# An unused 160-byte tile moves the expert stage's token tiles to the split weights' address modulo 512

## The chip, the cores and the metric

The kernel runs on one core of one Trainium2 chip. The metric is the device time of one execution in microseconds; the time before is the median of three runs. A core has 128 partitions of on-chip memory (SBUF), in which a tile has one byte address that holds for all partitions, and accumulators in PSUM. TensorE multiplies a stationary operand of 128x128, which a weight load (PEld in the profile) brings in, with a moving operand of up to 512 columns. VectorE is DVE in the profile, ScalarE ACT, SyncE SP; SyncE issues the loads from memory.

## The reference, cut to what matters

A decoder trunk of two layers over 256 tokens of width 1024, all in float32: a pooling mixer and a dense SwiGLU, then an attention mixer with shared keys and values and a mixture of experts, then a norm. The time is mostly in the mixture of experts. Every token goes to two of eight experts; each expert is a SwiGLU of hidden width 3584:

```python
hn = rmsnorm(h, ffn_norm[l])
logits = (hn @ w_router)
top_val, top_idx = lax.top_k(logits, 2)
gates = jax.nn.softmax(top_val, axis=-1)
# for each expert e, over the tokens x that chose it:
h_e = jax.nn.silu(x @ w_gate[e]) * (x @ w_up[e])      # 1024 -> 3584
y_e = h_e @ w_down[e]                                 # 3584 -> 1024
# y[token] += gate * y_e ; out = rmsnorm(h + y)
```

Three weight matrices of 1024 x 3584 float32 for each of eight experts, 352 MB in all, pass once through the core.

## The kernel before

**Precision by splitting.** TensorE multiplies in the reduced type float32r. Each operand is therefore split into a high part (a copy rounded by ScalarE, line 177) and a low part (the difference, by VectorE, line 181), and a product takes three matmuls: high weights with high tokens, high weights with low tokens (line 189), low weights with high tokens (line 192). `mm3` (lines 184 to 192) issues them, for several rows of 128 first all that use the high weights, then those with the low weights.

**Steps.** The work is a list of steps that `run()` (line 236) goes through. A step takes a piece of 128x1024 of a raw weight tile; `split_ahead` splits the pieces of the next three steps before a step's matmuls are issued. The high parts and the low parts have rings of four tiles of 4096 bytes each (`whp`, `wlp`), the raw tiles a ring of 11 tiles of 8192 bytes (`rawp`), to which in the last stage six slots in memory of finished stages are added (lines 751, 768, 770). A raw tile holds two pieces; `load` (line 156) issues its transfer of 1 MB on SyncE's queue as soon as its slot is free.

**Expert stage.** For each expert, `new_slots` (line 987) takes from the pool `m1` the tiles `xeH` and `xeL` (4096 bytes a partition each): the high and low parts of up to 128 of the expert's tokens, transposed, filled by `gather` (line 999) through a matmul with a one-hot. `expert` (line 1045) runs seven blocks of 512 hidden columns: four steps for gate, four for up, and, two blocks late, four steps for down. In a step (`moe_unit`, line 1024) the token tile is the stationary operand, 128x128, and the split weights are the moving operand, 512 columns: six matmuls, each with its own weight load. The hidden block is transposed (line 1054) and split into `hid` (three tiles of 4096 bytes in `m1`), which is the stationary operand of the down steps. After the last block the result goes back to the tokens by a matmul with the one-hot `ohT` (`scatter`, line 1065).

**Output projection.** In the attention stage `out_proj` (line 661) and `w_mm` (line 829) multiply with `w_o` in the same way: `oh` and `ol`, the merged heads transposed, are stationary, 128x128, and 512 columns of split weights are moving, again six matmuls in the order of `mm3`.

**Addresses.** Pools are laid out one after another, a tile's size is rounded up to 32 bytes. The pools on the left side end with those of the attention; `mp` (token tile `xm`, routing tiles of 64 bytes) and below it `m1` grow downwards from the top of the partition. The addresses in bytes, from the program as it is allocated: the four high weight tiles at 96032 and on by 4096, the low ones at 112416 and on, which is 288 modulo 512, as are all raw tiles; `oh` and `ol` of the output projection at 200480 and 202528, also 288 modulo 512; in `m1` `oh` 192960, `xeH` 193984, `xeL` 198080, `hid` 205248, 209344 and 213440, all 448 modulo 512, since each size in that pool is a multiple of 512; `xm` at 220608, also 448. The attention's largest tile ends at 192288, where `m1` would begin to collide. The pieces that a matmul reads lie at multiples of 512 bytes (stationary) or 2048 (moving) in their tiles, so a whole tile keeps one address modulo 512.

The order of the matmuls, loads and splits is that of the steps, written out; nothing in it depends on addresses, except that a tile waits for the tiles that had its memory before.

Of the kernel before, what the change touches and what calls it, by code (L numbers as in the profile page):

```python
# [12 lines left out]
F32 = mybir.dt.float32  # L13
# [24 lines left out]
P = 128  # L38
# [5 lines left out]
FE = 3584  # L44
NB = FE // 512
LAG = 2
EPS = 1e-6
NEG = -1e30
WINDOWS = (2, 4, 8, 16)
# [45 lines left out]
def trunk(ctx, tc, x, a_norm, a_proj, a_scale, kv_norm, w_kv, b_norm, w_q, w_o, rel_bias,  # L95
# [29 lines left out]
    def bankB(name):  # L125
        return psB.tile([P, 512], F32, tag="b", name=name)
# [20 lines left out]
    def flush():  # L147
        while pending:
            tick()
# [51 lines left out]
    def then(fn):  # L201
        steps.append((None, None, None, fn, None))
# [22 lines left out]
    def split_ahead(want):  # L225
        m = flow["now"]
        while m < len(steps) and want >= 0:
            raw_of, cut, name = steps[m][:3]
            if raw_of is not None:
                if m >= flow["reach"]:  # L230
                    flow["parts"][m] = split(cut(raw_of()), name) if name else (cut(raw_of()),)
                    flow["reach"] = m + 1
                want -= 1
            m += 1
# [38 lines left out]
    def rstd_of(ss, name):  # L273
        w = ss.shape[1]
        v = small.tile([P, 2], F32, tag="rv", name=f"rv_{name}")
        nc.vector.tensor_scalar(v[:, :w], ss, 1.0 / D, EPS, op0=ALU.mult, op1=ALU.add)
        r = cst.tile([P, 2], F32, name=f"rstd_{name}")
# [357 lines left out]
    def attend(b, h, i, prT, o):  # L635
        for s, (g, kt) in enumerate(SEG_KEYS[i]):
            nc.tensor.matmul(o, prT[:, s * P:(s + 1) * P], kvT["v", g][:, kt, h * 64:(h + 1) * 64],
                             start=(s == 0), stop=(s == 3))

    def merged(sm, on, i, pu):  # L640
        nc.vector.reciprocal(sm[:, i, :], sm[:, i, :])
        nc.vector.tensor_mul(on[:, i], pu.rearrange("p (h d) -> p h d", h=4),
                             sm[:, i, :].unsqueeze(2).to_broadcast([P, 4, 64]))

    def merge_tiles(b, pool):
        on = pool.tile([P, 2, 4, 64], F32, tag="on", name=f"on{b}")
        oh = pool.tile([P, 2, T], F32R, tag="oh", name=f"oh{b}")
        ol = pool.tile([P, 2, T], F32R, tag="ol", name=f"ol{b}")
        return on, oh, ol

    def turn_merged(b, on, oh, ol, i):
        po = bankB(f"ps_oT{b}_{i}")
        uf = on[:, i].rearrange("p h d -> p (h d)")
        for j in range(2):
            nc.tensor.transpose(po[:, j * P:(j + 1) * P], uf[:, j * P:(j + 1) * P], ident)
        pov = po[:, :T].rearrange("p (j t) -> p j t", j=2)
        hi = oh[:, :, i * P:(i + 1) * P]
        nc.scalar.activation(hi, pov, AF.Copy)
        nc.vector.tensor_sub(ol[:, :, i * P:(i + 1) * P], pov, hi.bitcast(F32))
# [136 lines left out]
    def moe_pool(name, bufs, side, ctx=mo_ctx):  # L796
        return ctx.enter_context(tc.tile_pool(name=name, bufs=bufs, side=side, reuse_waits="tile"))

    def last_merge():
        flush()  # L800
        split_ahead(3)
        pU = [bankB(f"ps_U3_{i}") for i in range(2)]
        on, oh, ol = mo["o"] = merge_tiles(3, av["one"])

        def att(h, i):
            attend(3, h, i, prev["probs"][h, i], pU[i][:, h * 64:(h + 1) * 64])

        for h in range(4):
            att(h, 0)
        merged(prev["sm"], on, 0, pU[0][:, :T])  # L810
        for h in range(3):
            att(h, 1)
        turn_merged(3, on, oh, ol, 0)
        att(3, 1)
        merged(prev["sm"], on, 1, pU[1][:, :T])
        late_ctx.close()
        mp = mo["mp"] = moe_pool("mp", 1, "right")
        mo["xm"] = mp.tile([P, 2, D], F32, name="xm")
        mo["ss"] = mp.tile([P, 2, 2], F32, name="ss_m")
        for nm in ("sel", "both", "gat", "pos"):  # L820
            mo[nm] = mp.tile([P, 2, NE], F32, name=nm)
        spare = av["big"][:, 4096:]
        mo["grow"], mo["sq"] = spare[:, :D], spare[:, D:D + 512]
        mo["h2T"] = {(n, i): av["at"].tile([P, 4, P], F32, tag="lg", name=f"h2T{n}_{i}", bufs=4)
                     for n in range(2) for i in range(2)}

    then(last_merge)

    def w_mm(wh, wl, n, i):
# [215 lines left out]
    def expert(e, got, sfx, next_expert=None):  # L1045
# [31 lines left out]
        def hidden_block(b):  # L1077
            nm = f"{sfx}{e}_{b}"
            ps = {}

            def acc(w):
                def f():
                    if w not in ps:
                        ps[w] = bankA(f"ps_m{w}{nm}")
                    return ps[w]
                return f

            def gate_done():
                hs = ps["h"] = mo["m1"].tile([P, 512], F32, tag=f"hs{b % 2}", name=f"hs{nm}")
                nc.scalar.activation(hs, ps["g"], AF.Silu)  # L1090

            def up_done():
                nc.vector.tensor_mul(ps["h"], ps["h"], ps["u"])
                later(TL if b == NB - 1 and next_expert is None else TURN, lambda: turn_hidden(ps["h"], b))

            for w, src, fn in (("g", moe_gate, gate_done), ("u", moe_up, up_done)):
                for kh in range(2):
                    moe_unit(src[e, kh * 512:(kh + 1) * 512, b * 512:(b + 1) * 512], acc(w),
                             lambda: (got()[1], got()[2]), 4 * kh, kh == 0, kh == 1, f"m{w}{nm}_{kh}",
                             fn if kh == 1 else None)  # L1100
# [10 lines left out]
        def down_unit(b, n):  # L1111
            def acc():
                if n not in hid:
                    hid[n] = psC.tile([P, 512], F32, tag="a", name=f"ps_y{sfx}{e}_{n}")
                return hid[n]

            src = moe_down[e, b * 512:(b + 1) * 512, n * 512:(n + 1) * 512]
            name = f"md{sfx}{e}_{n}_{b}"
            post = (lambda: y_done(n)) if b == NB - 1 else None
            if b in full:  # L1120
                native_unit(src, acc, lambda: hidden[b], b == NB - 1, name, post)
            else:
                moe_unit(src, acc, lambda: hidden[b], 0, b == 0, b == NB - 1, name, post)

        for b in range(NB):
            hidden_block(b)
            if b >= LAG:
                for n in range(2):
                    down_unit(b - LAG, n)
        if next_expert is not None:  # L1130
            then(next_expert)
        rest = [(b, n) for b in range(NB - LAG, NB) for n in range(2)]
        if next_expert is None:
# [5 lines left out]
    def square_out(n, i):  # L1139
# [5 lines left out]
        if n == 0:  # L1145
            nc.gpsimd.tensor_scalar(mo["part"][:, i:i + 1], mo["sso"][:, 0, i:i + 1], 1.0 / D, EPS,
                                    op0=ALU.mult, op1=ALU.add)
# [96 lines left out]
```

## Time and profile before

| | |
|---|---|
| median of three runs | 1567.74 us |
| the runs | 1566.62, 1567.74, 1570.31 us |
| span of the profiled execution | 1566.3 us (its own time beyond the span isn't listed; the fastest run is 1566.62 us) |
| granted clock, mean | 0.995 |
| busy: TensorE, VectorE, ScalarE | 98%, 76%, 64% |
| moved from and to memory | 441 MB, 282 GB/s over the span |

The profile is of one execution. Matmuls overlap, so the duration of one (some 395 ns with 512 columns) is longer than the distance to the next; the distance is read from the starts in the timeline, or from the number of matmuls in a window that is full. The timeline merges instructions of one kind that follow each other into one row with a count. The expert stage's steps begin near 542 us and end near 1552 us; the output projections run at 331, 408 and 484 us, with 24 matmuls each, and in smaller groups at 524 to 531 us.

### The profile page before, as it was taken

The numbers are of one execution on the slowest core, as the hardware profiler recorded it, in microseconds if no ns is written. First come the engines' busy times: TensorE is split into PE (matmuls) and PEld (weight loads), VectorE is DVE, ScalarE is ACT, GpSimd is POOL, SyncE is SP. The second block draws the span as 40 slices with busy tenths as digits, with TensorE's granted clock in tenths as the row PEclk, the third lists the DMA queues.
The fourth block names the chain that finished last, engine by engine and source line by source line (L and its number), as shares of the span: only waits on it lengthen the run. The fifth ranks groups of instructions, "written<-read, shape, count | busy, mean of one in ns | idle before, by whom it ended". The sixth has DMA issues, their size and how long they took to land. (4 is left out here: it accounts for less than half of the span.)

```text
span 1566.3 us, 22560 instructions
## 1 busy us (share of the span) xinstructions
PE 1541.6 (98%) x8849; PEld 1335.6 (85%) x8849; DVE 1198.2 (76%) x1346; ACT 1007.2 (64%) x1206; POOL 9.0 (1%) x16
## 2 busy tenths in 40 slices
PE   8999999999999999999999999999999999999996
PEld 7999999999999988888888888888888888888884
DVE  6666565354545598899888889888889888888984
ACT  5444445444444577777777767777777777777773
POOL 0000000000000000000000000000000000000001
PEclk9999999999999999999999999999999999999998
DMA  9955685646463799999989999999999999999930
GB/s 301 310 168 174 191 213 163 168 135 168 135 170 134 276 353 368 368 314 372 365 312 363 360 331 349 367 334 349 353 362 330 360 366 323 351 372 323 365 120 29
DMA packets 274803, 441.08 MB, mean 282 GB/s; under 512 B 28720, under 2 KB 100656, under 8 KB 274688
## 3 DMA queue, kind: packets, MB, share of 16 engines
q1 hardware_dynamic: 252448, 433.11, 79.6%
q10 hardware_dynamic: 22240, 6.45, 2.9%
q8 instruction: 71, 1.16, 0.3%
q14 instruction: 44, 0.36, 0.1%
HBM read 438.36 MB, written 1.17 MB: 281 GB/s over the span
## 5 line engine op out<-in xcount | busy, mean ns | idle before, releaser
L181 DVE TENSOR_TENSOR wl_mu<-raw_mu,wh_mu 128x1024 fp32r<-128x1024 f32 x196 | 233.2, 1220 | 41.0 <-ACT wh_mu L177 41.0
L181 DVE TENSOR_TENSOR wl_mg<-raw_mg,wh_mg 128x1024 fp32r<-128x1024 f32 x204 | 244.0, 1221 | 14.9 <-ACT wh_mg L177 13.8
L189 PE MATMUL ps_y<-wh_md,hid 128*128 128x512 f32 x880 | 242.7, 397 | 0.0
L177 ACT ACTIVATE wh_mg<-raw_mg 128x1024 fp32r<-128x1024 f32 x204 | 213.3, 1059 | 38.6 <-PE ps_y L189 24.6
L181 DVE TENSOR_TENSOR wl_md<-raw_md,wh_md 128x1024 fp32r<-128x1024 f32 x190 | 223.1, 1219 | 1.0 <-ACT wh_md L177 1.0
L177 ACT ACTIVATE wh_mu<-raw_mu 128x1024 fp32r<-128x1024 f32 x196 | 204.0, 1056 | 23.2 <-PE ps_mg L189 20.7
L177 ACT ACTIVATE wh_md<-raw_md 128x1024 fp32r<-128x1024 f32 x190 | 195.4, 1057 | 29.7 <-PE ps_mu L189 19.2
L189 PEld LDWEIGHTS ps_y<-wh_md,hid 128*128 128x128 f32 x880 | 164.1, 188 | 38.8 <-issue 0.5
L189 PE MATMUL ps_mg<-wh_mg,xeH 128*128 128x512 f32 x448 | 180.7, 403 | 0.0
L189 PE MATMUL ps_mu<-wh_mu,xeH 128*128 128x512 f32 x448 | 178.7, 399 | 0.0
L189 PE MATMUL ps_mg<-wh_mg,xeL 128*128 128x512 f32 x448 | 176.8, 395 | 0.0
L189 PE MATMUL ps_mu<-wh_mu,xeL 128*128 128x512 f32 x448 | 176.5, 394 | 0.0
L192 PE MATMUL ps_mu<-wl_mu,xeH 128*128 128x512 f32 x448 | 140.7, 395 | 0.0
L192 PE MATMUL ps_mg<-wl_mg,xeH 128*128 128x512 f32 x448 | 140.5, 394 | 0.0
L192 PE MATMUL ps_y<-wl_md,hid 128*128 128x512 f32 x440 | 137.9, 394 | 0.0
L192 PEld LDWEIGHTS ps_mu<-wl_mu,xeH 128*128 128x128 f32 x448 | 84.1, 188 | 20.8
L192 PEld LDWEIGHTS ps_mg<-wl_mg,xeH 128*128 128x128 f32 x448 | 84.1, 188 | 20.7
L189 PEld LDWEIGHTS ps_mu<-wh_mu,xeL 128*128 128x128 f32 x448 | 84.1, 188 | 19.6
L189 PEld LDWEIGHTS ps_mu<-wh_mu,xeH 128*128 128x128 f32 x448 | 84.1, 188 | 19.5
L189 PEld LDWEIGHTS ps_mg<-wh_mg,xeL 128*128 128x128 f32 x448 | 84.2, 188 | 18.5
L192 PEld LDWEIGHTS ps_y<-wl_md,hid 128*128 128x128 f32 x440 | 82.6, 188 | 20.4
L189 PEld LDWEIGHTS ps_mg<-wh_mg,xeH 128*128 128x128 f32 x448 | 84.2, 188 | 18.3
(244 smaller groups left out, 2712.6 us busy)
## 6 DMA issues: line engine op xcount, KB each, us to landing
raw_mg<-in_moe_w_gate_dram SPq DMA_DIRECT2D x102, 1024.0 KB, 7.1
raw_mu<-in_moe_w_up_dram SPq DMA_DIRECT2D x98, 1024.0 KB, 6.8
raw_md<-in_moe_w_down_dram SPq DMA_DIRECT2D x96, 1024.0 KB, 7.1
big<-in_moe_w_down_dram SPq DMA_DIRECT2D x16, 1024.0 KB, 7.1
big<-in_moe_w_up_dram SPq DMA_DIRECT2D x14, 1024.0 KB, 6.5
raw_k<-in_w_kv_dram SPq DMA_DIRECT2D x12, 1024.0 KB, 5.3
raw_q<-in_w_q_dram SPq DMA_DIRECT2D x12, 1024.0 KB, 5.5
raw_v<-in_w_kv_dram SPq DMA_DIRECT2D x12, 1024.0 KB, 5.3
```

The lines of the kernel that those rows point to most:

```text
L177: nc.scalar.activation(hv, raw, AF.Copy)
L181: nc.vector.tensor_sub(lv, raw, hv.bitcast(F32))
L189: nc.tensor.matmul(o, a, b, start=start and k == 0 and m == 0, stop=False)
L192: nc.tensor.matmul(o, a, b, start=False, stop=stop and k == n - 1)
```

## The change

A tile of 160 bytes that nothing reads or writes is taken from the pool `mp`, behind the routing tiles. The pool begins 160 bytes lower, and with it `xm` and the whole of `m1`: `xeH` goes from 193984 to 193824, `xeL` to 197920, `hid` to 205088, 209184 and 213280, which is 288 modulo 512, the split weights' own. No other address moves except routing tiles of `mp`, and no instruction is added.

```diff
@@ -44,6 +44,7 @@
 FE = 3584
 NB = FE // 512
 LAG = 2
+PHASE_FILL = 160
 EPS = 1e-6
 NEG = -1e30
 WINDOWS = (2, 4, 8, 16)
@@ -819,6 +820,7 @@
         mo["ss"] = mp.tile([P, 2, 2], F32, name="ss_m")
         for nm in ("sel", "both", "gat", "pos"):
             mo[nm] = mp.tile([P, 2, NE], F32, name=nm)
+        mp.tile([P, PHASE_FILL // 4], F32, name="fill")
         spare = av["big"][:, 4096:]
         mo["grow"], mo["sq"] = spare[:, :D], spare[:, D:D + 512]
         mo["h2T"] = {(n, i): av["at"].tile([P, 4, P], F32, tag="lg", name=f"h2T{n}_{i}", bufs=4)
```

## Rows read from the trace of the kernel before

**Rows 1.** the page: span, and busy time of each engine

```profile
span 1566.3 us, 22560 instructions
...
PE 1541.6 (98%) x8849; PEld 1335.6 (85%) x8849; DVE 1198.2 (76%) x1346; ACT 1007.2 (64%) x1206; POOL 9.0 (1%) x16
```

**Rows 2.** windows: busy us (instructions) by engine, clock, DMA share, GB/s

```profile
100.00:200.00 100.00, 100.00 (x835) 100.00 (x834) 60.87 (x68) 45.98 (x57) 0.00 (x0) 1.00 0.59 185
600.00:700.00 100.00, 100.00 (x461) 81.41 (x460) 88.20 (x88) 74.23 (x82) 0.00 (x0) 1.00 0.99 350
...
1200.00:1300.00 100.00, 100.00 (x460) 81.40 (x459) 87.57 (x86) 74.72 (x82) 0.00 (x0) 1.00 1.00 358
```

**Rows 3.** waits of TensorE, 750 to 1560 us: total, times, longest

```profile
PE ps_z L1068 <- ACT y L1106: 0.7, 1, 0.7
```

**Rows 4.** groups by line, TensorE, 542 to 1556 us: count, busy us, mean ns

```profile
L189 PE MATMUL ps_y<-wh_md,hid 128*128 128x512 f32 x880 | 242.7, 397 | 0.0
L189 PE MATMUL ps_mg<-wh_mg,xeH 128*128 128x512 f32 x448 | 180.7, 403 | 0.0
...
L192 PE MATMUL ps_y<-wl_md,hid 128*128 128x512 f32 x440 | 137.9, 394 | 0.0
L1054 PE MATMUL ps_hT<-misc,hs 128*128 128x128 f32 x224 | 33.5, 272 | 0.0
L1006 PE MATMUL ps_x<-oh,xm 128*128 128x128 f32 x230 | 28.1, 275 | 0.0
L1068 PE MATMUL ps_z<-y,ohT 128*128 128x512 f32 x32 | 13.7, 430 | 0.7 <-ACT y L1106 0.7
...
L1021 PE MATMUL ps_oh<-misc,oh 128*128 128x128 f32 x16 | 3.0, 271 | 0.0
```

**Rows 5.** timeline of TensorE, expert stage, starts of steps: start, us

```profile
640.85 0.40 PE L189 MATMUL ps_mu<-wh_mu,xeH 128*128 128x512 f32 x1
...
646.45 0.40 PE L189 MATMUL ps_y<-wh_md,hid 128*128 128x512 f32 x1
...
1510.46 0.40 PE L189 MATMUL ps_mu<-wh_mu,xeH 128*128 128x512 f32 x1
...
1513.27 1.10 PE L189 MATMUL ps_y<-wh_md,hid 128*128 128x512 f32 x4
```

**Rows 6.** timeline of TensorE, output projection, three steps

```profile
485.54 0.39 PE L189 MATMUL ps_o<-wh_o,oh 128*128 128x512 f32 x1
...
489.62 0.28 PE L189 MATMUL ps_v<-wh_v,akH 128*128 128x256 f32 x1
```

**Rows 7.** windows over two projections and four expert steps, columns as before

```profile
332.21:336.29 4.08, 4.08 (x19) 3.38 (x18) 3.66 (x5) 1.06 (x1) 0.00 (x0) 1.00 0.33 114
...
485.54:489.62 4.08, 4.08 (x20) 3.38 (x18) 3.65 (x5) 1.06 (x1) 0.00 (x0) 1.00 1.04 387
640.85:646.45 5.60, 5.60 (x25) 4.51 (x24) 4.64 (x5) 4.76 (x6) 0.00 (x0) 1.00 1.03 375
```

**Rows 8.** timeline of TensorE, projection after a break

```profile
330.82 0.40 PE L189 MATMUL ps_o<-wh_o,oh 128*128 128x512 f32 x1
...
332.21 0.39 PE L189 MATMUL ps_o<-wh_o,oh 128*128 128x512 f32 x1
...
526.17 0.40 PE L189 MATMUL ps_o<-wh_o,ol 128*128 128x512 f32 x1
...
527.32 0.39 PE L189 MATMUL ps_o<-wh_o,oh 128*128 128x512 f32 x1
...
529.35 0.40 PE L189 MATMUL ps_o<-wh_o,ol 128*128 128x512 f32 x1
...
530.06 0.62 PE L192 MATMUL ps_o<-wl_o,oh 128*128 128x512 f32 x2
```

**Rows 9.** waits of SyncE's load queue: total us, times, longest

```profile
SPq L162 <- DVE wl_mg L181: 321.7, 107, 18.2
```

## The prediction

> **What bounds the kernel now.** I read the page first: the span is 1566.3 us and TensorE is busy for 1541.6 us of it [rows 1]. Then the table of 100 us windows: from 600 us on TensorE is busy for the whole of each window at a granted clock of 1.00, its 2.4 GHz level, while VectorE has 88% and ScalarE 75%; the 16 DMA engines stand at 0.99 to 1.00 [rows 2]. That looks like two bounds at once, so I asked for the waits. Between 750 and 1560 us TensorE's longest wait is one of 0.7 us, in the tail [rows 3]: the expert stage, about 542 to 1552 us, is a row of matmuls that wait for no semaphore. What its time depends on is then the spacing of the matmuls themselves. The list by line says how many there are: six kinds of 448, one of 880 and one of 440, that is 2688 + 880 + 440 = 4008 matmuls of 512 columns, each with a weight load of its own [rows 4].
>
> The timeline gives the spacing. A step is six such matmuls, four with the high weights and two with the low ones. From 640.85 to 646.45 us lie four steps, 5.60 / 4 = 1.400 us each, or 233.3 ns a matmul; two steps near the stage's end take 2.81 us, the same within rounding [rows 5].
>
> The attention stage holds the same step in another place: the output projection also loads a 128x128 pair of token tiles and streams 512 columns of split weights, in the same order (high, low, high, low, then two low weights). There three steps take 489.62 - 485.54 = 4.08 us, 1.360 us each or 226.7 ns a matmul [rows 6]. Nothing waits in either. What differs by layout: in the projection the token tiles (200480 and 202528) and the split weights (96032 and on by 4096) all start at 288 modulo 512; in the expert stage the token tiles start at 448, the weights at 288. The change makes both 288.
>
> **What else differs between the two.** The windows over both say how far the comparison holds [rows 7]. The projection at 332 us ran with the DMA engines at 0.33, the one at 485 us with 1.04 and 387 GB/s, more than the expert stage's 375; both took 4.08 us. So DMA traffic isn't the cause. VectorE is busy 90% there and 83% in the expert stretch, so neither is VectorE. ScalarE is busy 26% there against 85%; that one isn't excluded by these rows.
> A third point supports the reading: in 100 to 200 us 835 matmuls, nearly all of 256 columns, run in 100 us, 119.8 ns each [rows 2]; their token tiles and weights also share the phase 288. Between 119.8 and 226.7 ns lie 256 columns, 0.418 ns each, which leaves 12.9 ns a matmul. The expert stage's 233.3 ns lies 6.6 ns above that line.
>
> **The change, part by part.**
> The unused tile has no instruction and no DMA, so nothing is added to a queue. It takes 160 bytes below the position tile; everything of the expert pool moves down by 160, from 192960 to 192800 at its lower end, and the attention tensors under it end at 192288, so it fits. Each moved tile still lies over the same attention tiles as before (the high token tile, 193984 to 198080 before and 193824 to 197920 after, lies over the three value tiles both times), so no wait is added or lost at the stage's start. I cost this at 0; nothing has to hide it.
> The token tiles, the hidden tiles and the scatter's one-hot all have sizes that are multiples of 512, so all of them get the phase 288. For the matmuls of 512 columns the pair (weight load, moving operand) goes from 448 against 288 to 288 against 288. Taking the projection's spacing: 4008 / 6 = 668 steps by 1.400 - 1.360 = 0.040 us, 26.7 us.
> From that comes off what each break costs. The row of matmuls is broken by 224 / 4 = 56 groups of hidden transposes, 14 gathers of 16, 8 one-hot turns and about 28 scatters before the tail [rows 4], some 106 in all, and in the projection the spacing of 226.7 ns is reached only some matmuls after a break: from 330.82 to 332.21 us six took 1.39 us, 0.03 more than 1.36; after a transpose five took 527.32 - 526.17 = 1.15, 0.02 more than 1.133 [rows 8]. I take 0.025, 106 x 0.025 = 2.7 us. Bounds: 0 where the expert stage settles at once, 106 x 0.040 = 4.2 us where a whole step's gain is lost at every break.
> Transposes, gathers and scatters: gather and scatter have both operands in the expert pool, which move together, so their difference stays; the transposes take the identity from another phase before and after. No row shows a 128-column pair at the new difference; their groups have means of 272 and 275 ns before [rows 4], and a shift of 2 ns either way on some 480 is 1 us either way. I take 0.
> The gain is 26.7 - 2.7 = 24.0 us, from 22.5 to 26.7, with 1 us either way.
>
> **What is late next.** TensorE's stage shrinks by 24 of some 1010 us. VectorE's 88 to 90% becomes at most 92%, ScalarE's 75% becomes 77%: both stay below TensorE. DMA must go from 350 to 350 x 1010 / 986 = 359 GB/s. That is close to what it has reached, but the load queue waits for slots, not slots for it: its longest waits by total are on VectorE's release of a raw tile, 321.7 us over 107 issues for the gate weights alone [rows 9], and no row of the stage's waits has a weight split waiting for a DMA. With up to 17 slots (11 of the ring, six lent by other pools) at two steps each, a tile is loaded some 40 us ahead; a shortfall of 1% over 900 us, 9 us, is covered by that.
>
> **Sum.** The profiled span is 1566.3 us; the runs gave 1566.62 to 1570.31 with a median of 1567.74, 1.4 us above the span. Span 1566.3 - 24.0 = 1542.3, with the 1.4 us 1543.7.
>
> **The rivals.**
> Phase is not the cause. Against the forecast stands ScalarE's different load, and that the phases were not varied within one stage. Then the spacing stays 1.400 us and the time 1567.7, within 0.2% (3 us, about what a measurement of this kernel can tell from no change). The same holds if the shift does not reach the operands.
> The Trainium skill speaks for this one: SBUF — State Buffer, Who interferes with whom, gives TensorE two read ports of its own and says that "PE and ACT never wait on anyone", and TensorE: Matmul & The Clock Gate, Step-by-step: what each phase is for, says that loading the next weights does not take read bandwidth from the running matmul. By that an address could not matter and the time would be 1567.7 us; the trace does not agree or disagree outright, but it shows two spacings for one instruction pair, 226.7 and 233.3 ns [rows 5, 6], where that page's Back-to-back issue gap has one of about 216 ns.
> The gain is met by the next limit, the transfer of the weights. From 600 to 700 us the DMA share is 0.99 at 350 GB/s [rows 2]; read as a limit of 350 / 0.99 = 353.5 GB/s, the stage could speed up by 1.0% of 1010 us, 10 us, if no lead were left: 1557.7. With the lead of 40 us the missing 14 us are covered, so the case lies between 1543.7 and 1557.7. Against it: 358 GB/s in another window, 387 over 4 us [rows 7], and the lead.
> Slower. The pair can also run in a worse pattern at equal phase: after the transposes at 529 us three matmuls of the projection took 530.06 - 529.35 = 0.71 us, 236.7 ns each [rows 8], and that burst ended before it settled. If the expert stage, broken 106 times and with ScalarE busier, stays in such a pattern, 4008 x (236.7 - 233.3) = 13.6 us are added: 1581. It decides from 233.3 ns a matmul on. Against: the projections at 332 and 485 us hold 226.7 for three steps each [rows 7].
>
> **Chances.** Forecast 0.80, own range 1540 to 1547; next limit 0.06; no change 0.09; slower 0.05. Faster is 0.80 + 0.06 = 0.86. The range goes from 1539 (the full 26.7 us, 1 us from the transposes and a median 1 us nearer the span) to 1552, more than half of the way to 1557.7; so it leaves out no change, slower and about half of the limit's case, 0.17.
>
> **What would show it.** Right: in the expert stage a step of 1.36 us on the timeline, some 471 instead of 460 matmul records in 100 us, DMA near 359 GB/s there, the stage's start at 542 us unmoved, attention steps still 1.36. Wrong: steps of 1.400 us (phase is no cause), steps of 1.42 (the worse pattern), or steps of 1.36 with gaps in TensorE's row that wait for a split weight (the next limit).

## The result, and the profile after

The changed kernel takes 1544.26 us in the median of four runs (1542.15 to 1546.35), the kernel before 1567.18 (four runs, 1566.39 to 1570.31): a ratio of 0.9845, 95% interval 0.983 to 0.986, 22.9 us less. The forecast was 1543.7.

The page of the profiled execution, which took 1544.2 us itself, with the span and the busy time of each engine:

```profile
span 1542.4 us, 22560 instructions
...
PE 1517.8 (98%) x8849; PEld 1335.7 (87%) x8849; DVE 1194.1 (77%) x1346; ACT 1007.2 (65%) x1206; POOL 9.0 (1%) x16
```

The same number of instructions on every engine, and the same work on ScalarE to the tenth of a microsecond; the span is 23.9 us shorter and TensorE's busy time 23.8 us [rows 1]. So it is TensorE's own time that went, not a wait. The windows of the kernel after (busy us and instructions of PE, PEld, DVE, ACT, POOL; granted clock, DMA share, GB/s) say in which stage:

```profile
100.00:200.00 100.00, 100.00 (x835) 100.00 (x835) 60.90 (x68) 45.99 (x57) 0.00 (x0) 1.00 0.57 185
600.00:700.00 100.00, 100.00 (x469) 83.29 (x468) 90.15 (x90) 77.30 (x85) 0.00 (x0) 1.00 0.99 357
...
1200.00:1300.00 100.00, 100.00 (x470) 83.34 (x469) 90.51 (x90) 76.22 (x83) 0.00 (x0) 1.00 0.99 357
```

In the dense stage as many matmuls as before, in the expert stage 469 and 470 instead of 461 and 460 in a window that was full both times, at the same granted clock of 1.00, the 2.4 GHz level [rows 2]. DMA moves 357 GB/s, near the 359 of the prediction. The timeline of TensorE (start, us, then the instructions), at the stage's start, over one block of up steps, and over the first down steps with a break between:

```profile
542.15 0.47 PE L190 MATMUL ps_mg<-wh_mg,xeH 128*128 128x512 f32 x1
...
639.63 0.39 PE L190 MATMUL ps_mu<-wh_mu,xeH 128*128 128x512 f32 x1
...
640.99 0.39 PE L190 MATMUL ps_mu<-wh_mu,xeH 128*128 128x512 f32 x1
...
643.71 1.07 PE L190 MATMUL ps_y<-wh_md,hid 128*128 128x512 f32 x4
...
645.07 1.07 PE L190 MATMUL ps_y<-wh_md,hid 128*128 128x512 f32 x4
...
646.43 1.07 PE L190 MATMUL ps_y<-wh_md,hid 128*128 128x512 f32 x4
...
647.79 1.07 PE L190 MATMUL ps_y<-wh_md,hid 128*128 128x512 f32 x4
...
649.15 0.60 PE L1056 MATMUL ps_hT<-misc,hs 128*128 128x128 f32 x4
649.51 1.18 PE L190 MATMUL ps_y<-wh_md,hid 128*128 128x512 f32 x4
...
650.98 1.09 PE L190 MATMUL ps_y<-wh_md,hid 128*128 128x512 f32 x4
```

Every step from 639.63 to 649.15 us takes 1.36 us, up and down alike: 9.52 / 7. It was 1.40 [rows 5]. After the four transposes the first step takes 1.47. The projection keeps its 1.36 [rows 6], (488.06 - 485.34) / 2:

```profile
485.34 0.39 PE L190 MATMUL ps_o<-wh_o,oh 128*128 128x512 f32 x1
...
488.06 0.39 PE L190 MATMUL ps_o<-wh_o,oh 128*128 128x512 f32 x1
```

The groups by line (count, busy us, mean ns) from 542 to 1556 us, answering to rows 4, show which instructions changed:

```profile
L190 PE MATMUL ps_y<-wh_md,hid 128*128 128x512 f32 x880 | 237.2, 391 | 0.0
L190 PE MATMUL ps_mg<-wh_mg,xeH 128*128 128x512 f32 x448 | 178.4, 398 | 0.0
...
L193 PE MATMUL ps_y<-wl_md,hid 128*128 128x512 f32 x440 | 135.8, 390 | 0.0
L1056 PE MATMUL ps_hT<-misc,hs 128*128 128x128 f32 x224 | 33.5, 272 | 0.0
```

The 512-column groups shown became 4 to 6 ns shorter a matmul; the transposes have 33.5 us as before [rows 4]. A matmul's duration overlaps its neighbours', so the saving is not the count times the change of the mean; the start-to-start distance is what adds up. The stage has 3907 distances between 512-column matmuls of gate, up and down with nothing between them; read from all starts, they go from 917.8 to 894.7 us, 23.2 us less before rounding.

Last, the waits: TensorE's between 750 and 1560 us and SyncE's longest (total us, times, longest).

```profile
PE ps_z L1070 <- ACT y L1108: 0.7, 1, 0.7
PE ps_z L1071 <- DVE y L1109: 0.2, 1, 0.2
```

```profile
SPq L163 <- DVE wl_mg L182: 311.2, 107, 18.4
```

No wait for a split weight has come; the load queue still waits for slots, on this release 10 us less than before [rows 3, 9]. The next limit wasn't met.

### The profile page after: what moved, and what is told of

It reads as the page before. It is cut to its first block, busy times and chain, and to the rows that moved or that the text cites. A ratio compares the mean times of both kernels' runs of the same rounds, so it can differ in the third digit from the quotient of the medians.

```text
span 1542.4 us, 22560 instructions
## 1 busy us (share of the span) xinstructions
PE 1517.8 (98%) x8849; PEld 1335.7 (87%) x8849; DVE 1194.1 (77%) x1346; ACT 1007.2 (65%) x1206; POOL 9.0 (1%) x16
## 5 line engine op out<-in xcount | busy, mean ns | idle before, releaser
L190 PE MATMUL ps_y<-wh_md,hid 128*128 128x512 f32 x880 | 237.2, 391 | 0.0
L178 ACT ACTIVATE wh_md<-raw_md 128x1024 fp32r<-128x1024 f32 x190 | 195.4, 1058 | 23.5 <-PE ps_mu L190 14.4
```

The source lines that it names most:

```text
L178: nc.scalar.activation(hv, raw, AF.Copy)
L190: nc.tensor.matmul(o, a, b, start=start and k == 0 and m == 0, stop=False)
```

## Experiments

Theory: the distance between two 512-column matmuls, each with a weight load, depends on the difference of the start addresses of their stationary and moving operands modulo 512. Rivals: one absolute address is good; the position of one operand alone decides; ScalarE's load decides; the modulus is another. Each kernel ran once, beside the kernel before, unless the text says otherwise. Distances are means over the neighbouring starts of one kind (gate, up or down) in the expert stage, those under 260 ns; the stage's length is from the start of the first gate matmul to that of the last down matmul: 1007.1 us before, 983.4 after. The stage's start lay between 541.0 and 545.4 us among these kernels. It goes with how long TensorE's granted clock stood at 0.5, its 1.2 GHz level, in the stages before: not at all in the earliest, 3.4 us in those that start at 542.1 to 542.8, 6.8 us at 543.3 to 544.3 and 10.2 us in the latest. So the length is the better measure.

**Move the other operand.** The kernel before, with the split weights laid out ahead of the small tiles, so that they start at 448, where the token tiles are. In the projection the pair is then unequal, 288 against 448.

```diff
+    first = ctx.enter_context(tc.tile_pool(name="first", bufs=2))
+    whp = ctx.enter_context(tc.tile_pool(name="whp", bufs=4))
+    wlp = ctx.enter_context(tc.tile_pool(name="wlp", bufs=4))
     small = ctx.enter_context(tc.tile_pool(name="small", bufs=2))
     rawp = ctx.enter_context(tc.tile_pool(name="rawp", bufs=RING))
-    whp = ctx.enter_context(tc.tile_pool(name="whp", bufs=4))
-    wlp = ctx.enter_context(tc.tile_pool(name="wlp", bufs=4))
...
```

> The token tiles stay at 448 modulo 512 as before; the split weights are moved to 448 instead (they are laid out ahead of the small tiles; the raw tiles and all others keep 288). Theory, the difference of the two addresses modulo 512 decides: the expert stage's step is 1.360 us and that stage ends some 23 us earlier; the output projection, now 288 against 448, loses its 1.360, and the stages of 256 columns may lose some of their 119.8 ns a matmul, so that the time lies above 1544 us. Rival, the address of the token tiles by itself decides (288 is good, 448 is bad): the step stays 1.400 us, the projection stays 1.360, the time stays near 1567 us.

It took 1545.26 us (before: 1567.39), stage length 983.2. Its window and, on the timeline, four step starts in the projection:

```profile
600.00:700.00 100.00, 100.00 (x471) 83.39 (x470) 89.63 (x90) 76.96 (x85) 0.00 (x0) 1.00 0.99 357
```

```profile
485.08 0.40 PE L190 MATMUL ps_o<-wh_o,oh 128*128 128x512 f32 x1
...
486.49 0.39 PE L190 MATMUL ps_o<-wh_o,oh 128*128 128x512 f32 x1
...
487.89 0.40 PE L190 MATMUL ps_o<-wh_o,oh 128*128 128x512 f32 x1
...
489.29 0.40 PE L190 MATMUL ps_o<-wh_o,oh 128*128 128x512 f32 x1
```

The expert stage gained as with the change, and the projection lost what the expert stage had won: 4.21 / 3 = 1.403 us a step. The two stages changed places while ScalarE had the same work (1007.5 us in all, 1007.2 before), so neither ScalarE nor an absolute address explains it. And the dense stages' 256-column pairs, now 160 apart, run as before:

```profile
100.00:200.00 100.00, 100.00 (x835) 100.00 (x834) 61.80 (x68) 44.94 (x56) 0.00 (x0) 1.00 0.57 183
```

835 matmuls in 100 us both ways [rows 2]. Their distances now spread from 116 to 125 ns where they were 120, but the mean is 120.0 in the dense stage's down part both ways: at 256 columns a difference of 160 changes the pattern and costs nothing. The attention's value matmuls, also of 256 columns but with the weights as the moving operand, 352 apart in this kernel, even ran faster: 117.7 ns instead of 119.7, 1.0 us in all.

**Move only the gate and up tokens.** The 160 bytes lie between the token tiles of the first expert's slots and the tiles allocated after them, so that `xeH` and `xeL` are at 288 and `hid` stays at 448.

```diff
         got.append(new_slots(0, ""))
+        mo["m1"].tile([P, 40], F32, name="fill")
```

> The 160 bytes are put into the expert pool behind the first expert's token tiles: the token tiles of gate and up go to 288, the hidden tiles, the stationary operand of the down steps, stay at 448. Theory, each matmul pays for its own pair: gate and up steps 1.360 us, down steps 1.400 us; of the 23 us two thirds come, 2688 / 4008 x 23.2 = 15.6 us, 1551.5 us. Rival, one kind of tile carries it all (or a change of the pool's other tiles does): either all 23 us, 1544, or none, 1567.

1555.69 us (before: 1567.39), stage length 992.8. Its timeline, two up steps and two down steps:

```profile
643.74 0.39 PE L189 MATMUL ps_mu<-wh_mu,xeH 128*128 128x512 f32 x1
...
645.10 0.39 PE L189 MATMUL ps_mu<-wh_mu,xeH 128*128 128x512 f32 x1
...
646.47 1.09 PE L189 MATMUL ps_y<-wh_md,hid 128*128 128x512 f32 x4
...
647.87 1.09 PE L189 MATMUL ps_y<-wh_md,hid 128*128 128x512 f32 x4
```

Side by side within ten microseconds, 1.36 for up and 1.40 for down: 227.7 and 227.5 ns against 233.4. The distances of gate and up sum to 13.9 us less than before, against 14.3 with the whole change, and those of down to 0.2 more; the stage is 14.4 us shorter. The time is 4.2 us above the expected 1551.5; the stage started 2 us later and gained 1.2 us less than the 15.6 expected.

**Other amounts.** The change with another size of the unused tile: 672 (512 more), 96, 128, 192, 416 and 32 bytes.

```diff
-PHASE_FILL = 160
+PHASE_FILL = 672   # and 96, 128, 192, 416, 32, each a kernel
```

> The unused tile has 672 bytes, 160 + 512. Theory, the difference modulo 512 decides: same as with 160 bytes, steps of 1.360 us, 1544 us. Rival, the distance or a larger modulus (1024 or 2048 bytes) decides: steps of another length, and a time away from 1544 us.

> The unused tile has 96 bytes: token tiles at 352, weights at 288, difference 64. Theory in its narrow form, only a difference of 0 modulo 512 is good: steps of some 1.40 us, 1567 us. Rival, a smaller modulus decides (64 bytes): steps of 1.360 us, 1544 us. In between: the surcharge depends on the difference step by step, and the step lies between 1.36 and 1.40 us.

> The unused tile has 128 bytes: token tiles at 320, weights at 288, a difference of 32, the least that the layout allows. Theory, only a difference of 0 is good: 233.2 ns a matmul as at 64 and 160, 1567 us. Rival, the surcharge grows with the difference: between 226.7 and 233.2 ns, some 1548 to 1560 us.

> The unused tile has 192 bytes: token tiles at 256, weights at 288, a difference of -32 (480 modulo 512). Theory, only 0 is good: 233.2 ns, 1567 us. Rival, the sign matters (the tokens that lie behind the weights are late, those ahead are not): 226.7 ns or less here, 1544 us or less.

> The unused tile has 416 bytes: token tiles at 32, weights at 288, a difference of 256, as far away as it gets modulo 512. Theory, only 0 is good: 233.2 ns, 1567 us. Rival, a modulus of 256 decides: 226.7 ns, 1544 us. Second rival, the farther the better or worse: away from 233.2 ns in either direction.

> The unused tile has 32 bytes: token tiles at 416, weights at 288, a difference of 128. After the run with a difference of 256 the modulus is 256 or a divisor of it. Theory, the modulus is 256: 233.2 ns a matmul, 1567 us. Rival, it is 128 (differences of 160, 64, 32, 96 and 224 are all no multiples of 128, so no run so far speaks against it): 226.7 ns, 1544 us.

The difference is stationary less moving start, modulo 512. Distances are of gate, up and down.

| bytes | difference | time, us (before beside it) | distances, ns | stage, us |
|---|---|---|---|---|
| 0 | 160 | 1567.18 | 233.2, 233.2, 233.2 | 1007.1 |
| 32 | 128 | 1567.73 (1568.1) | 233.1, 233.2, 233.4 | 1006.5 |
| 96 | 64 | 1569.51 (1567.39) | 233.1, 233.1, 233.2 | 1007.2 |
| 128 | 32 | 1567.64 (1569.97) | 233.2, 233.2, 233.3 | 1006.6 |
| 160 | 0 | 1544.26 (1567.18) | 227.8, 227.2, 226.9 | 983.4 |
| 192 | 480 | 1567.29 (1569.97) | 233.0, 233.1, 233.3 | 1006.3 |
| 416 | 256 | 1546.33 (1569.97) | 227.8, 227.2, 226.9 | 983.4 |
| 672 | 0 | 1547.71 (1567.39) | 227.7, 227.2, 226.9 | 983.4 |

The windows of 416 and of 32 bytes, the two whose answer decides the modulus:

```profile
600.00:700.00 100.00, 100.00 (x471) 83.28 (x470) 89.61 (x91) 76.30 (x85) 0.00 (x0) 1.00 1.00 360
```

```profile
600.00:700.00 100.00, 100.00 (x461) 81.48 (x460) 88.20 (x88) 74.33 (x82) 0.00 (x0) 1.00 0.98 351
```

471 matmuls in the window at a difference of 256, 461 at 128. It is all or nothing: 32 bytes off on either side loses the whole gain, 256 off loses none. My theory of a modulus of 512 falls; a modulus of 256 fits all eight rows, and 128 is excluded by the row of 32 bytes. Not one of the other sizes beats the change: 416 and 672 have its stage length, and the stage starts 2 and 3 us later.

**The short pairs.** The change, and the identity tile, which the hidden transposes load or stream, moved from 128 to 288 as well, so that their pair is equal too.

```diff
+    first = ctx.enter_context(tc.tile_pool(name="first", bufs=2))
...
-    mhalf = cst.tile([P, 2], F32, name="mhalf")
+    mhalf = first.tile([P, 2], F32, name="mhalf", bufs=1)
```

> On top of the change the constant tile with the identity is moved from 128 to 288 modulo 512, so that the transposes of the hidden blocks have both operands at 288 as well; the weights and the token tiles stay at 288. If a pair of 128 columns pays for its difference too, the 168 distances of 108.8 ns within the transposes fall, by at most 1 us in all per 6 ns, and the first distances behind a break (some 315 ns and then 231 to 236 ns) may shorten: 1 to 2 us, 1542.5 us. If, as with 256 columns, short pairs do not pay: 1544 us, no change.

1545.5 us (1542.6 to 1546.46, four runs) against 1569.97 for the kernel before: ratio 0.9843 (0.9826 to 0.9859), the change's own. The transposes' group is the one after, to the digit:

```profile
L1057 PE MATMUL ps_hT<-misc,hs 128*128 128x128 f32 x224 | 33.5, 272 | 0.0
```

Start to start they take 108.6 ns, 108.8 in the change and 108.6 in the kernel before, where the pair is unequal. For these transposes of 128 columns equal addresses bring nothing.

**Only the low token tile apart.** The change with two more unused tiles around `xeL`, which alone goes back to 448; of the six matmuls of a gate or up step, the second and the fourth then have an unequal pair.

```diff
+        if not got:
+            m1.tile([P, 40], F32, name="fill1")
         xeL = m1.tile([P, NK, P], F32R, tag="xeL", name=f"xeL{sfx}{e}")
+        if not got:
+            m1.tile([P, 88], F32, name="fill2")
```

> With the change, and two further unused tiles in the expert pool: the low token tiles of gate and up alone go back to 448, the high ones and all others stay at 288. In a gate or up step two of six matmuls then have a difference of 160. Theory, each matmul pays for itself: steps of 1.360 + 2 x 0.0066 = 1.373 us in gate and up, 1.360 in down, 1544 + 2688 / 4008 x 23.2 / 3 = 1549 us. Rival, the pattern is one of the whole row, and a third of foreign pairs breaks it: steps of 1.400 us in gate and up, 1559.6 us.

1555.25 us (before: 1568.1), stage length 995.6. Its timeline, three up steps and two down steps:

```profile
639.83 0.40 PE L190 MATMUL ps_mu<-wh_mu,xeH 128*128 128x512 f32 x1
...
644.00 1.08 PE L190 MATMUL ps_y<-wh_md,hid 128*128 128x512 f32 x4
...
645.38 1.07 PE L190 MATMUL ps_y<-wh_md,hid 128*128 128x512 f32 x4
646.74 1.07 PE L190 MATMUL ps_y<-wh_md,hid 128*128 128x512 f32 x4
```

An up step takes 4.17 / 3 = 1.39 us, a settled down step 1.36. Over the 306 unbroken gate and up steps the six distances, from the first matmul on, are 233.8, 231.6, 231.7, 231.7, 233.3 and 227.5 ns; in the change they are 226.7 to 227.6. So the distance into an unequal pair is long, and so are the two that follow the last of them; only the sixth is as short as in the change. A third of the pairs brings (1389.7 - 1362.1) / (1399.9 - 1362.1) = 0.73 of the surcharge. That each matmul pays for its own pair falls, and the rival, that one foreign pair spoils the whole step, is nearer but not exact.

## Why the prediction was right, point by point

**What bounds.** Right: TensorE's row waits for nothing and the time is in its spacing. Nearly all of the gain is there: the stage is 23.7 us shorter, of 23.9 in the span.

**The step, 26.7 us.** Right in mechanism: 1.400 to 1.360 us, from the projection, and the exchange of the two stages by moving the weights shows that the pair, not the stage, makes the difference. Of the 3834 distances outside the breaks, 3459 are now 224 to 228 ns, 3380 of them 226 or 227. The term was a little large: those 3834 were 233.24 ns each before and not 233.33, 0.4 us in all, and of the 4008 matmuls 174 lie next to a break, where 0.8 us came back instead of 1.2.

**The breaks, 2.7 us.** The 3834 distances take 871.4 us, 2.3 us more than at 226.67 ns each: 375 of them still lie at 229 to 236. The term was 0.4 us too large, and that it came so near is in part luck: the prediction spread it evenly over some 106 breaks, but 2.0 of the 2.3 us lie behind the 56 groups of transposes, 35 ns each, and 0.15 us behind the 28 scatters, 5 ns each. The 73 longest distances, nearly all the first after a break, are no part of the 3834; they fell from 23.6 to 23.3 us. So the spacings of all 3907 gave 23.2 us back; the stretches across the breaks, from the last such matmul before to the first one behind, gave 0.5, most of it at the scatters. That is the stage's 23.7 us, where 24.0 were forecast.

**Transposes, gathers, scatters, 0 ± 1 us.** Right: 33.5 us for the transposes before and after, and they stay so with an equal pair; the 0.5 us across the breaks lie within the range.

**What lies around the span.** I added 1.4 us, the median less the span. The profiled run after has 1544.2 - 1542.4 = 1.8. The span was forecast to 0.1 us, 1542.3 against 1542.4; this 0.4 us and a median that lies 0.06 above the profiled run make the difference. That the span came out so near is luck as well: 0.2 of its 23.9 us are the stage's earlier start, 542.15 instead of 542.35 us, to which the change adds nothing.

**The third point was wrong.** I read the 256-column matmuls as a third pair that equal phase makes fast. They run at the same spacing, 835 in 100 us, when they are 160 apart. The line through the two points was no evidence, and the expert stage's 6.6 ns above it was a coincidence of sizes. The forecast didn't rest on it.

**Modulo 512** was narrower than need be: 256 apart does as well.

**The rivals.** Phase no cause: gone with the first step of 1.36 us. By the Trainium skill, SBUF — State Buffer, Who interferes with whom, TensorE never waits on anyone, and by the Trainium skill, TensorE: Matmul & The Clock Gate, Step-by-step: what each phase is for, the next weight load takes no read bandwidth from the running matmul. The runs disagree with what the prediction drew from these sentences, that an address could not matter: with ScalarE's work the same and DMA at 357 instead of 350 GB/s, the address of one operand of TensorE relative to its other one decided between 233.3 and 226.7 ns, 3%. The 216 ns that the prediction sets beside these two stand in the Trainium skill, TensorE: Matmul & The Clock Gate, Back-to-back issue gap, for an isolated matmul and not for a row with a weight load each; no run here shows them. The next limit: DMA went to 357 GB/s without a wait. The worse pattern at equal phase: 236 ns does occur, but only for some matmuls after a break.

**Open.** Which two accesses meet isn't settled: a matmul's own weight load and its stream, or the next weight load and the stream that is running; in most of these kernels both change together. The trace of the kernel with only the gate and up tokens moved speaks for the second: at its 40 unbroken changes from up to down, the last up matmul has an equal pair of its own, but the distance from it to the first down matmul, whose stationary tile is 160 apart, is 236.7 ns; the distance just ahead is 226.9, and with the whole change the same one is 226.6. That isn't the whole account, since in the last experiment two distances behind the last unequal pair are long too. Why the period is 256 bytes isn't shown either. Differences under 32 bytes were not tried, since tile sizes are rounded to 32.

## What to carry to other kernels

Where TensorE's row is full, waits for nothing and loads new weights for every 512-column matmul, compare the start-to-start distance between stages; two values for the same shape are a reason to compare the operands' start addresses. Put the stationary and the moving tile at the same address modulo 256, with an unused tile if need be, and put every stationary tile of the row there: one of two apart kept 0.73 of the loss. Such a fill is worth trying by itself, as it has no instruction. At 256 columns and for the transposes of 128 equal addresses brought nothing here, and the value matmuls ran 2 ns faster with unequal ones.

## What the runs showed of the hardware that was not expected

- Where all pairs have the same difference, its effect has two levels and nothing between: 227 ns at 0 or 256 bytes, 233 at 32, 64, 128, 160 and 480.
- The mean of the slow level is one, its pattern is not: at a difference of 160 the distances repeat in threes (237, 231, 232 ns), at 64 and 32 in twos (231 or 232 and 235). The mean stays at 233.2 within 0.2 ns.
- After the hidden transposes of 128 columns, five or ten distances between 512-column matmuls pass in the changed kernel until the short one is steady, at a granted clock of 1.00 throughout; after the 21 scatters without a transpose beside them the first distance is 226 or 227 ns already.
- Four of the kernels (slots alone, 128, 416, 672 bytes) have a stretch of 3.4 us in the attention's key projection, which no fill touches, between 295.8 and 303.0 us, at a granted clock of 0.5, the 1.2 GHz level. There 256-column matmuls are 213 ns apart instead of 120, which costs 1.4 us. In all twelve kernels TensorE had waited for a split weight just before, 1.5 to 2.1 us in these four and 1.2 to 1.6 us in the others, so the wait alone does not say why only four lost the clock.
